# Hybrid encoder block with a mixture of experts: a slice-ordered copy of x2, and a row bound on the gathers and scatters

## The chip, the core and the metric

The kernel runs on one core of a Trainium2 chip. TensorE (PE in the rows) multiplies matrices, with a weight load (PEld) for the stationary operand of each product; VectorE (DVE), ScalarE (ACT) and GpSimd (POOL) work elementwise; SyncE (SP) issues transfers; sixteen DMA engines move data between HBM and the on-chip memory. The metric is the device time of one launch, the median of several runs, in microseconds (us).

## The reference

One encoder layer over 512 tokens of width 1024, all in float32:

```python
h = rmsnorm(x, norm_mix_w[l])
proj = h @ w_in[l]
...
merged = g_attn * (attn @ w_attn_o[l]) + g_ssd * (ssd @ w_ssd_o[l])
x = x + merged @ w_out[l]                     # called x2 below
h2 = rmsnorm(x, norm_ffn_w[l])
x = x + hierarchical_moe(h2, ...)
...
def hierarchical_moe(h, w_rg, b_rg, w_re, b_re, w1, w3, w2):
    p_group = softmax(t @ w_rg + b_rg); g_val, g_idx = top_k(p_group, 1)
    fine_sel = ...                            # the 4 expert logits of the group
    e_val, e_idx = top_k(softmax(fine_sel), 2)
    ...
    for e in range(16):
        y_e = (silu(t @ w1[e]) * (t @ w3[e])) @ w2[e]
        out = out + combine[:, e:e + 1] * y_e
```

Each token goes to one group of four experts and to two experts in it, so 1024 pairs of token and expert are to be computed. An expert has w1 and w3 of 1024 x 512 and w2 of 512 x 1024, 96 MB of weights over all sixteen.

## The kernel before

**Up to x2.** Input projection, attention, the two-way state-space part, the gates and the output projection come first. The last of it is `wout_mm`, after which `x2_add` (L1361) forms x2 in four blocks of 128 tokens, each in two halves. The sum's squares (`x2_sq`, L1364, ScalarE) give the norm's factor. For the router, `u_t` (L1369, TensorE) transposes a half block of x2, `u_out` (L1376, ScalarE) copies it out, `logits` (L1384, TensorE) multiplies it with the router's weights, `lg_copy` and `lg_sum` (L1387 to L1392) add the parts up, and `topk` (L1409 to L1444, VectorE) picks the experts. `pos_mm` and `base_mm` (L1446 to L1457) count the tokens ahead of each, which gives every pair of token and expert a slot.

**Slots.** Each expert has 96 slots, in three parts r of 32. The sixteen experts run in four rounds q, four experts (4j + q) at a time, so that a part of a round is 128 rows: 32 slots of each of four experts. `s_oh` (L1644) builds one-hot matrices of tokens against slots, `s_mm` multiplies them with a table of token numbers and factors, `s_ix` (L1663) turns the result into row numbers for the gathers, and `s_ti` (L1672 ff.) into factors and into row numbers for the scatters. An empty slot gathers row 0 and scatters to a spare row behind the 512 tokens, for which the output has 128 rows more.

**The first round's first part** isn't gathered. `oh_first` (L1473, VectorE) makes one-hots, and `pg_first` (L1480 to L1483) multiplies x2, as the stationary operand, with them: 24 products, for blocks t = 0, 1, 2 and for eight k. The slice k of x2 is every eighth column. `first_out` (L1703, L1706) puts the product into TH, the transposed tokens of the experts.

**The other eleven parts** are gathered by rows from h_d (called h2_d in the code), the copy of x2 in HBM that `h2_store` (L1400) writes; `gather` (L1685, GpSimd) fills GS or GX, `turn` (L1692, TensorE) transposes every eighth column at a time, `turned` (L1698, L1703) copies out.

**The experts.** `up_mm` (L1718) makes pu with w1 and pv with w3, `g_silu` and `g_mul` (L1741, L1745) join them, `turn` transposes, `down_mm` (L1726) multiplies with w2, `y_ev` (L1896, L1898) scales, `scatter` (L1748, GpSimd) adds the 128 rows of a part to the output in HBM. x2 itself was stored there first by `x2_store` (L1403). The phases run u0 v0 u1 w0 v1 u2 w1 v2 u3 w2 v3 w3 (u for w1, v for w3, w for w2, then the round). A part that would need more than 96 slots is done in an overflow loop, which these inputs don't enter.

**The weights** come as 192 loads of 512 KB (`eload`, L1750 to L1753, SyncE), in a fixed order, into 33 buffers: 21 of their own and 12 (EXu, EXx, EXr) that are made out of memory which other work leaves. A load waits in SyncE's queue until its buffer is free.

**What sets the order.** A planner in the program (class `Plan`) schedules all jobs of TensorE, VectorE, ScalarE, GpSimd and SyncE before the launch, by priorities, dependencies and prices that are written in the code, and the program is emitted in that order.

Of the kernel before, what the change touches and what calls it, by code (L numbers as in the profile page):

```python
# [217 lines left out]
def tile_block(ctx: ExitStack, tc: tile.TileContext, x, norm_mix_w, w_in, b_gate, q_norm_w, k_norm_w,  # L218
# [350 lines left out]
    spare = cp.tile([P, 1], F32, name="spare")  # L569
    tsb = cp.tile([P, P], BF16, name="tsb")  # L570

    def router_c():
# [903 lines left out]

    def pg_first(t, kb, js):
# [181 lines left out]
    def s_ix(nm, q, rs):  # L1659
# [3 lines left out]
        V.tensor_scalar(ix[q][:, a:b], pi_(nm)[:, a:b, 0], 0.0, None, op0=ALU.add)  # L1663
        V.tensor_tensor(ix[q][:, a:b], ix[q][:, a:b], pi_(nm)[:, a:b, 1], op=ALU.add)
    ix, ti, sx, ri = {}, {}, {}, {}

# [379 lines left out]
```

## Time and profile before

| | us |
|---|---|
| median of 3 runs | 672.26 (670.43 to 672.67) |
| profiled execution | 671.2 |
| its span in the profile | 669.4 |
| TensorE busy | 651.3 |
| VectorE busy | 321.5 |
| ScalarE busy | 240.7 |
| GpSimd busy | 83.0 |

The span is the time between the first and the last recorded work; the execution's own time holds some 2 us more around it. TensorE's clock was granted in full up to the last matmuls. The page shows shares of busy time over the whole span, and since the stages differ, the rows that follow are taken from single stages: the first-round products from 370 to 384 us, the experts from 384 to 657, and the last scatter. The columns are told with each group.

### The profile page before, as it was taken

What the parts mean: (1) busy time and instruction counts of PE and PEld (TensorE: products, weight loads), DVE (VectorE), ACT (ScalarE), POOL (GpSimd) and SP (SyncE); (2) the same over time, 40 slices, a digit from 0 to 9 for tenths busy, and PEclk for the clock granted to TensorE, in tenths of its full rate; (3) what the DMA queues carried; (4) which work ended last, traced back from release to release, by engine and by line L of the source; (5) the groups of instructions that cost most, each with busy time, mean ns of one, the idle gap of its engine ahead of it and who ended that gap; (6) DMA issues with size and microseconds to landing.
All of it is one profiled execution on the core that took longest, in us unless ns stands there. A gap on an engine that the chain in (4) does not pass through costs nothing. (4 is left out here: it accounts for less than half of the span.)

```text
span 669.4 us, 11417 instructions
## 1 busy us (share of the span) xinstructions
PE 651.3 (97%) x4616; PEld 401.0 (60%) x4618; DVE 321.5 (48%) x677; ACT 240.7 (36%) x441; POOL 83.0 (12%) x110
## 2 busy tenths in 40 slices
PE   7999999999999999999999999999999999999982
PEld 5888887777788888888877833443334333333320
DVE  4779868987698997566433580420112011001100
ACT  5444555777567778633442110001100110011100
POOL 5434100222000000000002020110010001000111
PEclk9999999999999999999999999999999999999997
DMA  8732632564221112698754579999999999999934
GB/s 287 183 86 44 179 94 66 141 205 127 64 64 32 32 33 64 206 324 318 285 187 175 204 224 317 419 418 418 406 366 386 418 398 373 386 417 386 368 89 65
DMA packets 79612, 154.85 MB, mean 231 GB/s; under 512 B 8696, under 2 KB 45060, under 8 KB 79556
## 3 DMA queue, kind: packets, MB, share of 16 engines
q1 hardware_dynamic: 70692, 131.27, 53.7%
q0 software_dynamic: 6800, 22.76, 12.7%
q8 instruction: 37, 0.61, 0.4%
q10 hardware_dynamic: 2064, 0.07, 0.2%
q14 instruction: 19, 0.16, 0.1%
HBM read 143.48 MB, written 10.58 MB: 230 GB/s over the span
## 5 line engine op out<-in xcount | busy, mean ns | idle before, releaser
L271 PE MATMUL b<-hTh,wc_hi 128*128 128x512 f32 x208 | 85.4, 410 | 0.0
L273 PE MATMUL b<-hTh,wc_lo 128*128 128x512 f32 x208 | 82.2, 395 | 0.0
L272 PE MATMUL b<-hTl,wc_hi 128*128 128x512 f32 x208 | 82.2, 395 | 0.0
L1718 PE MATMUL pu<-u,TH 128*32 128x512 f32 x600 | 74.5, 593 | 0.0
L1726 PE MATMUL py<-w,GS 128*32 128x512 f32 x456 | 71.5, 592 | 1.7 <-DMA w<-in_w_dram 1.7
L1718 PE MATMUL pv<-v,TH 128*32 128x512 f32 x456 | 69.0, 593 | 0.0
L1896 DVE TENSOR_SCALAR YS<-py,ti 128x512 f32<-128x512 f32 x12 | 9.0, 751 | 116.8 <-PE py L1726 116.4
L271 PEld LDWEIGHTS b<-hTh,wc_hi 128*128 128x128 f32 x208 | 39.1, 188 | 10.2 <-issue 1.5
L669 DVE TENSOR_TENSOR wc_lo<-wc_r,wc_hi 128x1024 fp32r<-128x1024 f32 x34 | 41.5, 1223 | 7.7 <-ACT wc_hi L665 7.5
L1698 ACT ACTIVATE GS<-pts 128x512 f32<-128x512 f32 x12 | 6.6, 597 | 106.9 <-PE pts L1692 106.9
L273 PEld LDWEIGHTS b<-hTh,wc_lo 128*128 128x128 f32 x208 | 39.1, 188 | 9.4
L665 ACT ACTIVATE wc_hi<-wc_r 128x1024 fp32r<-128x1024 f32 x34 | 35.8, 1056 | 24.4 <-PE b L272 14.9
L1718 PEld LDWEIGHTS pu<-u,TH 128*32 128x32 f32 x600 | 20.5, 110 | 39.1 <-issue 37.0
L272 PEld LDWEIGHTS b<-hTl,wc_hi 128*128 128x128 f32 x208 | 39.2, 188 | 7.7
L1726 PEld LDWEIGHTS py<-w,GS 128*32 128x32 f32 x456 | 19.4, 110 | 39.0 <-issue 33.2
L1748 POOL DMA_INDIRECT out_dram<-YS,sx x12 | 18.7, 1559 | 190.1 <-DVE YS L1896 132.4
L1718 PEld LDWEIGHTS pv<-v,TH 128*32 128x32 f32 x456 | 18.6, 110 | 29.7 <-issue 27.9
L1703 DVE TENSOR_TENSOR TH<-ptt,nfc 128x512 f32<-128x512 f32 x21 | 13.2, 684 | 46.3 <-PE ptt L1692 46.3
L1898 ACT ACTIVATE YS<-py,ti 128x512 f32<-128x512 f32 x12 | 8.3, 688 | 69.4 <-PE py L1726 69.1
L1745 DVE SCALAR_TENSOR_TENSOR YS<-pv,ri,YS 128x512 f32<-128x512 f32 x8 | 6.0, 751 | 56.1 <-PE pv L1718 55.9
L1718 PE MATMUL pv<-EXr,TH 128*32 128x512 f32 x108 | 32.1, 593 | 0.0
L1741 ACT ACTIVATE YS<-pu,ri 128x512 f32<-128x512 f32 x8 | 5.5, 688 | 62.8 <-PE pu L1718 56.3
(367 smaller groups left out, 1393.3 us busy)
## 6 DMA issues: line engine op xcount, KB each, us to landing
u<-in_w_dram SPq DMA_DIRECT2D x50, 512.0 KB
v<-in_w_dram SPq DMA_DIRECT2D x38, 512.0 KB
w<-in_w_dram SPq DMA_DIRECT2D x38, 512.0 KB
wc_r<-in_w_in_dram SPq DMA_DIRECT2D x26, 512.0 KB
EXu<-in_w_dram SPq DMA_DIRECT2D x24, 512.0 KB
EXr<-in_w_dram SPq DMA_DIRECT2D x22, 512.0 KB
EXx<-in_w_dram SPq DMA_DIRECT2D x20, 512.0 KB
x<-in_x_dram SPq DMA_DIRECT2D x8, 512.0 KB
```

Source lines behind the costliest of these rows:

```text
L271: T.matmul(ps, lhsT=lh, rhs=rh, start=first, stop=False)
L272: T.matmul(ps, lhsT=lh, rhs=rl, start=False, stop=False)
L273: T.matmul(ps, lhsT=ll, rhs=rh, start=False, stop=last)
L665: A.activation(t_["w", i][0], t_["raw", i], AF.Copy)
L669: V.tensor_tensor(l_, t_.pop(("raw", i)), h_.bitcast(F32), op=ALU.subtract)
L1698: A.activation(sT_(g[2]), i, AF.Copy)
L1703: V.tensor_tensor(o, i, nfc[:, k0:k0 + 4].unsqueeze(2).to_broadcast([P, 4, P]), op=ALU.mult)
L1718: T.matmul(t_["p", x_, q, r][js, :], lhsT=T_(q, r)[:, k, js], rhs=t_["raw", x_, q, k // 2, j][:, k % 2, :], start=k == 0, stop=k == KD - 1)
L1726: T.matmul(t_["p", h, q, r][js, :], lhsT=sT_(r)[:, k, js], rhs=t_["raw", "w", q, k, j].rearrange("p a n -> p (a n)")[:, int(h) * 512:(int( ...
L1748: G.indirect_dma_start(out, bass.IndirectOffsetOnAxis(ap=sx[q][:, r:r + 1], axis=0), y_buf(r), None, compute_op=ALU.add)
L1896: V.tensor_scalar(o, i, w_, None, op0=ALU.mult)
L1898: A.activation(o, i, AF.Copy, scale=w_)
```

## The change

- `u_w` is new: ScalarE copies x2 into a buffer us of the same size with the columns put in slice order (slice k contiguous), eight copies of 128 x 512.
- `pg_first` takes its stationary operand from us, in contiguous slices; the planner's price of a pair of products goes from 0.51 to 0.29.
- `h2_store` stores us instead of x2, so that gathered rows are in slice order, and `turn` reads them contiguously.
- The table of token numbers has NONE = 4096 taken off, and `s_ix` adds it back, so that an empty slot has a row number above 511. Gathers and scatters get a bound of 511 for the row, beyond which a row is left out. The scatters use the gathers' row numbers; the spare rows, their numbers and the output's extra rows are gone.
- `clear` is new: three memsets on GpSimd of the buffers into which the gathers write, ahead of the first gather.
- The planner gets other priorities (`oh_first` earlier, the second round's slots later), and the buffers that are made out of freed memory are others: us takes the place of two of them, and the two halves of each lp come in.

```diff
-        c[:, C_TC + 2 * t + 1] = t * P
+        c[:, C_TC + 2 * t + 1] = t * P - NONE
...
+    def u_w(t, nh):
+        A.activation(us(t).rearrange("n (k p) -> n k p", k=KD)[:, :, nh * 64:nh * 64 + 64],
+                     x2(t)[:, nh * 512:(nh + 1) * 512].rearrange("n (p k) -> n k p", k=KD), AF.Copy)
+
     def h2_store(t):
-        G.dma_start(h2_d[t * P:(t + 1) * P, :], x2(t))
+        G.dma_start(h2_d[t * P:(t + 1) * P, :], us(t))
...
-            T.matmul(t_["pg", kb][:, j * P:(j + 1) * P], lhsT=x2(t).rearrange("n (p k) -> n k p", k=KD)[:, kb * 4 + j, :],
+            T.matmul(t_["pg", kb][:, j * P:(j + 1) * P], lhsT=us(t)[:, (kb * 4 + j) * P:(kb * 4 + j + 1) * P],
                      rhs=oh0()[:, t, :], start=False, stop=(t, j) == (NT - 2, 3))
...
+        w_ = job("act", 0.65, lambda: u_w(t, nh), [j_] + j_x2, prio=prio + (2 if t < NT - 1 or nh == 0 else 8))
...
-        j_ = job("dve", 0.17, lambda t=t: oh_first(t), [j_slot[t]], prio=PGP)
+        j_ = job("dve", 0.17, lambda t=t: oh_first(t), [j_slot[t]], prio=-1000)
...
+    def clear(r):
+        G.memset(g_buf(r), 0.0)
...
-        V.tensor_scalar(ix[q][:, a:b], pi_(nm)[:, a:b, 0], 0.0, None, op0=ALU.add)
+        V.tensor_scalar(ix[q][:, a:b], pi_(nm)[:, a:b, 0], float(NONE), None, op0=ALU.add)
...
-        st += [lambda: V.tensor_copy(fx, pi_(nm)[:, :, 0]),
-               lambda: V.tensor_tensor(fx, fx, pi_(nm)[:, :, 1], op=ALU.add),
-               lambda: V.reduce_sum(own, w_.rearrange("p r j i -> p r i j"), axis=AX.X),
-               lambda: V.reduce_sum(ti[q], own[:, :, 0:3], axis=AX.X),
-               lambda: V.scalar_tensor_tensor(fx, fx, spare[:, 0:1], own[:, :, 3], op0=ALU.subtract, op1=ALU.mult),
-               lambda: V.tensor_scalar(sx[q], fx, spare[:, 0:1], None, op0=ALU.add)]
+        st += [lambda: V.reduce_sum(own, w_.rearrange("p r j i -> p r i j"), axis=AX.X),
+               lambda: V.reduce_sum(ti[q], own[:, :, 0:3], axis=AX.X)]
...
-        G.indirect_dma_start(g, None, h2_d, bass.IndirectOffsetOnAxis(ap=i, axis=0))
+        G.indirect_dma_start(g, None, h2_d, bass.IndirectOffsetOnAxis(ap=i, axis=0), bounds_check=S - 1, oob_is_err=False)
...
-        src = g_buf(g[2]).rearrange("n (p k) -> n k p", k=KD) if g[0] == "t" else s_buf(g[2]).rearrange("n (k p) -> n k p", k=4)
+        src = g_buf(g[2]).rearrange("n (k p) -> n k p", k=KD) if g[0] == "t" else s_buf(g[2]).rearrange("n (k p) -> n k p", k=4)
...
-        G.indirect_dma_start(out, bass.IndirectOffsetOnAxis(ap=sx[q][:, r:r + 1], axis=0), y_buf(r), None, compute_op=ALU.add)
+        G.indirect_dma_start(out, bass.IndirectOffsetOnAxis(ap=ix[q][:, r:r + 1], axis=0), y_buf(r), None, bounds_check=S - 1,
+                             oob_is_err=False, compute_op=ALU.add)
...
+    for i, h, after in ((0, 1, [j_ra]), (0, 0, uts), (1, 0, uts + pgs + [j_w5, j_tab]), (1, 1, uts + pgs + [j_w5, j_tab])):
+        job("any", 0.0, lambda i=i, h=h: ebufs.append(
+            lambda nm, dt=F32, pat=None, **kw: lp[i][:, h * 1024:(h + 1) * 1024].rearrange(pat, **kw)), after, free=["e"], lat=0.0)
     for i in range(2):
-        more(g8, "EXx%d" % i, [j for t in (2 * i, 2 * i + 1) for n in range(2) for j in js[t][n]] + j_st[2 * i:2 * i + 2]
-             + j_h2[2 * i:2 * i + 2] + pgt[2 * i] + (pgt[1] if i == 0 else []))
-    more(a8, "EXr0", uts + [j_rooms])
-    more(a8, "EXr1", uts + pgs + [j_w5, j_tab, j_rooms])
+        more(g8, "EXu%d" % i, j_h2[2 * i:2 * i + 2] + (pgt[0] + pgt[1], pgt[2])[i])
...
-        o = (700, at["u", 0] + 8, at["v", 0] + 38, at["v", 0] + 39)[q]
+        o = (700, at["u", 0] + 32, at["v", 0] + 38, at["v", 0] + 39)[q]
```

On TensorE, the end of the first products before: pg_3644 and pg_3675 are the two halves of the products, x_0 and x_1 the blocks of x2, plt the router's sums, and pu the first up-product.

```order
L1480 MATMUL pg_3675<-zb,onb 128x512
L1482 MATMUL pg_3675<-lp_3257,x_0_3296 128x128 x4
L1384 MATMUL plt<-lp_3256,wr 32x128 x4
...
L1457 MATMUL plt<-mk,onb 128x16
L1482 MATMUL pg_3644<-lp_3257,x_0_3296 128x128 x4
L1392 MATMUL plt<-sel,lp_3257 128x20 x2
L1482 MATMUL pg_3675<-lp_3257,x_0_3296 128x128 x4
L1482 MATMUL pg_3644<-lp_3257,x_1_3299 128x128 x4
L1482 MATMUL pg_3675<-lp_3257,x_1_3299 128x128 x4
L1718 MATMUL pu_0_3742<-u_0_0_2920,TH_3650 32x512
```

The same place after the change, where the products are pg_3649 and pg_3669 and read us.

```order
L1488 MATMUL pg_3669<-lp_3255,us_3383 128x128 x2
L1371 MATMUL ph_3_1_3678<-cst,x_1_3298 128x128 x4
L1488 MATMUL pg_3669<-lp_3255,us_3383 128x128 x2
L1488 MATMUL pg_3649<-lp_3255,us_3383 128x128 x4
L1488 MATMUL pg_3669<-lp_3255,us_3383 128x128 x4
...
L1386 MATMUL plt<-lp_3254,wr 32x128 x4
L1488 MATMUL pg_3649<-lp_3255,us_3421 128x128 x2
L1394 MATMUL plt<-sel,lp_3255 128x20 x2
L1488 MATMUL pg_3649<-lp_3255,us_3421 128x128 x2
L1488 MATMUL pg_3669<-lp_3255,us_3421 128x128 x4
L1726 MATMUL pu_0_3746<-u_0_0_2918,TH_3655 32x512
```

More of the products now stand ahead of the last block's logits (L1386, L1384 before), and eight instead of sixteen behind them; nothing else changed places there.

On VectorE, between the third block's slots and the eviction of the first products (TH) before:

```order
L1460 TENSOR_SCALAR low<-plt 128x16
L1644 TENSOR_TENSOR oh_149<-cst,slot 128x384
L1644 TENSOR_TENSOR oh_150<-cst,slot 128x384
L1644 TENSOR_TENSOR oh_148<-cst,slot 128x384
L1406 SCALAR_TENSOR_TENSOR lp_3257<-plt,rs_141,prm 128x20
L1473 TENSOR_TENSOR lp_3257<-cst,slot 128x128
L1431 TENSOR_REDUCE lp_3257<-lp_3257 128x5
...
L1436 TENSOR_TENSOR lp_3257<-lp_3257 128x20
L1703 TENSOR_TENSOR TH_3650<-pg_3644,nfc 128x512
```

And after:

```order
L1467 TENSOR_SCALAR low<-plt 128x16
L1480 TENSOR_TENSOR lp_3255<-cst,slot 128x128
L1654 TENSOR_TENSOR oh_148<-cst,slot 128x384
L1654 TENSOR_TENSOR oh_149<-cst,slot 128x384
L1654 TENSOR_TENSOR oh_147<-cst,slot 128x384
L1413 SCALAR_TENSOR_TENSOR lp_3255<-plt,rs_140,prm 128x20
L1711 TENSOR_TENSOR TH_3655<-pg_3649,nfc 128x512
L1438 TENSOR_REDUCE lp_3255<-lp_3255 128x5
```

The third one-hot for the products (L1480, L1473 before) moved ahead of the three 128x384 one-hots, and the eviction into TH moved ahead of the last block's choice of experts.

On SyncE, the loads of the second half of v0 (w3 of the first round) before, by buffer:

```order
L1753 DMA v_0_2_3347<-in_w_dram 128x1024
L1347 DMA wt_3_r<-in_w_out_dram 128x2x512
L1753 DMA EXu_3363<-in_w_dram 128x1024 x2
L1753 DMA EXu_3387<-in_w_dram 128x1024 x2
L1753 DMA v_1_3_3418<-in_w_dram 128x1024
L1753 DMA v_2_0_3460<-in_w_dram 128x1024
L1753 DMA EXr_3716<-in_w_dram 128x1024 x2
L1753 DMA EXx_3740<-in_w_dram 128x1024 x2
L1753 DMA EXx_3777<-in_w_dram 128x1024 x2
L1753 DMA EXr_3838<-in_w_dram 128x1024 x2
```

And after, where EXx_3571 and EXu_3718 lie in the blocks of x2 and wait for the x2 stores, EXx_3762 and EXu_3814 lie in us and wait for the h2 stores and the products:

```order
L1349 DMA wt_3_r<-in_w_out_dram 128x2x512
L1762 DMA v_0_3_3354<-in_w_dram 128x1024
L1762 DMA v_1_0_3392<-in_w_dram 128x1024
L1762 DMA v_1_1_3458<-in_w_dram 128x1024
L1762 DMA EXx_3571<-in_w_dram 128x1024 x2
L1762 DMA EXu_3718<-in_w_dram 128x1024 x2
L1762 DMA EXx_3762<-in_w_dram 128x1024 x2
L1762 DMA lp_3254<-in_w_dram 128x1024
L1762 DMA EXu_3814<-in_w_dram 128x1024 x2
L1762 DMA lp_3255<-in_w_dram 128x1024 x2
```

Four loads (EXu_3363, EXu_3387) needed no late release before; now EXu_3718 and the seven loads behind it wait for the last block's stores or the products.

## Rows read from the trace of the kernel before

**Rows 1.** The page, busy us by engine, with share of span and instructions.

```profile
PE 651.3 (97%) x4616; PEld 401.0 (60%) x4618; DVE 321.5 (48%) x677; ACT 240.7 (36%) x441; POOL 83.0 (12%) x110
```

**Rows 2.** Windows of the expert stage: busy us (instructions) by engine, clock, DMA share, GB/s.

```profile
450.00:475.00 25.00, 25.00 (x237) 7.83 (x240) 1.71 (x3) 2.22 (x4) 1.78 (x2) 1.00 1.03 418
```

**Rows 3.** Waits of SyncE's queue, 400 to 640 us: total us, times, longest.

```profile
SPq L1753 <- PE pu L1718: 22.3, 7, 19.2
```

**Rows 4.** Timeline of TensorE near the end: start, us, instruction, count, idle before and releaser.

```profile
634.84 1.90 PE L1726 MATMUL py<-EXu,GS 128*32 128x512 f32 x16
637.04 1.04 PE L1726 MATMUL py<-w,GS 128*32 128x512 f32 x2 [0.30 <-DMA w<-in_w_dram]
639.52 1.05 PE L1726 MATMUL py<-w,GS 128*32 128x512 f32 x2 [1.43 <-DMA w<-in_w_dram]
640.76 1.04 PE L1726 MATMUL py<-EXr,GS 128*32 128x512 f32 x2 [0.20 <-DMA EXr<-in_w_dram]
642.00 0.62 PE L1726 MATMUL py<-EXr,GS 128*32 128x512 f32 x1 [0.19 <-SPq L2009]
```

**Rows 5.** Windows after the last matmul, columns as in rows 2.

```profile
661.00:665.00 4.00, 0.00 (x0) 0.00 (x0) 0.00 (x0) 0.00 (x0) 0.00 (x0) 0.64 0.86 131
665.00:669.40 4.40, 0.00 (x0) 0.00 (x0) 0.00 (x0) 0.00 (x0) 0.00 (x0) 0.50 0.00 0
```

**Rows 6.** Timeline of TensorE, first-round products to first transposes of gathered rows.

```profile
377.42 0.52 PE L1392 MATMUL plt<-sel,lp 128*128 128x20 f32 x4
377.78 5.99 PE L1482 MATMUL pg<-lp,x 128*128 128x128 f32 x24
383.70 0.64 PE L1718 MATMUL pu<-u,TH 128*32 128x512 f32 x4
...
399.10 0.71 PE L1692 MATMUL ptt<-cst,GS 128*128 128x128 f32 x4
```

**Rows 7.** Groups of weight loads over the span: busy us, mean ns, idle before.

```profile
L1482 PEld LDWEIGHTS pg<-lp,x 128*128 128x128 f32 x48 | 11.8, 334 | 0.0
L1392 PEld LDWEIGHTS plt<-sel,lp 128*128 128x128 f32 x16 | 2.3, 191 | 0.3
L1692 PEld LDWEIGHTS ptt<-cst,GS 128*128 128x128 f32 x56 | 6.8, 193 | 3.4 <-issue 3.4
L1692 PEld LDWEIGHTS pts<-cst,YS 128*128 128x128 f32 x32 | 3.4, 141 | 4.2 <-issue 2.5 <-DVE YS L1745 1.7
```

**Rows 8.** Timeline of TensorE: four contiguous transposes, eight strided ones, the next product.

```profile
440.05 0.60 PE L1692 MATMUL pts<-cst,GS 128*128 128x128 f32 x4
440.48 1.05 PE L1692 MATMUL ptt<-cst,GS 128*128 128x128 f32 x8
441.47 1.06 PE L1718 MATMUL pu<-u,TH 128*32 128x512 f32 x8
```

**Rows 9.** Timeline of VectorE beside the first products.

```profile
376.19 1.50 DVE L1644 TENSOR_TENSOR oh<-cst,slot 128x384 bf16<-128x384 f32 x3
...
381.89 0.69 DVE L1703 TENSOR_TENSOR TH<-pg,nfc 128x512 f32<-128x512 f32 x1 [2.20 <-PE pg L1482]
```

**Rows 10.** Timeline of ScalarE, one half block of x2: its squares, then the logits' copy.

```profile
364.22 0.63 ACT L1364 ACTIVATE lp<-x 128x512 bf16<-128x512 f32 x1 [1.20 <-DVE x L1361]
...
365.28 0.60 ACT L1376 ACTIVATE lp<-ph 128x512 f32<-128x512 f32 x1 [0.33 <-PE ph L1369]
```

**Rows 11.** Timeline of TensorE: the logits that read this copy.

```profile
366.56 0.43 PE L1384 MATMUL plt<-lp,wr 128*32 128x128 f32 x8
```

**Rows 12.** Timeline of GpSimd: the last store of x2 and the first gather.

```profile
372.09 0.53 POOL L1403 DMA_DIRECT2D out_dram<-x  x1
...
389.53 1.26 POOL L1685 DMA_INDIRECT GS<-h_d,ix  x1 [16.33 <-issue]
```

**Rows 13.** DMA issues by line: count, KB each, median us from issue to landing.

```profile
out_dram<-x POOLq DMA_DIRECT2D x4, 512.0 KB, 4.8
GS<-h_d,ix POOLq DMA_INDIRECT x7, 6.2
```

More of the change, by code (lines that the diff above doesn't have):

```diff
@@ L69 @@
 OFF = 2048
+NONE = 4096
 TG = ((0, 2), (2, 3), (3, 4))
@@ L1765, in tile_block @@
     j_rooms = job("any", 0.0, rooms, wo_all, lat=0.0)
[L1766 removed]
+    uts = [js[t][n][i] for t in range(NT) for n in range(2) for i in (2, 3)]
     pgs = pgj[0] + pgj[1]
     for i in range(2):
[L1769 removed]
+        more(g8, "EXx%d" % i, [j for t in (2 * i, 2 * i + 1) for n in range(2) for j in js[t][n]] + j_st[2 * i:2 * i + 2])
+    for i, h, after in ((0, 1, [j_ra]), (0, 0, uts), (1, 0, uts + pgs + [j_w5, j_tab]), (1, 1, uts + pgs + [j_w5, j_tab])):
+        job("any", 0.0, lambda i=i, h=h: ebufs.append(
+            lambda nm, dt=F32, pat=None, **kw: lp[i][:, h * 1024:(h + 1) * 1024].rearrange(pat, **kw)), after, free=["e"], lat=0.0)
     for i in range(2):
[L1771 to L1774 removed]
+        more(g8, "EXu%d" % i, j_h2[2 * i:2 * i + 2] + (pgt[0] + pgt[1], pgt[2])[i])
     phases = [("u", 0), ("v", 0), ("u", 1), ("w", 0), ("v", 1), ("u", 2), ("w", 1), ("v", 2), ("u", 3), ("w", 2), ("v", 3), ("w", 3)]
@@ L1786, in tile_block @@
                     [j_rq] + ([last["e"]] if "e" in last else []), ["e"], prio=1000 + len(jw), lat=DLAT)
+    jcl = [job("pool", 0.9, lambda r=r: clear(r), [j_rooms], prio=PL + 40 + r) for r in (1, 2, 0)]
     def sl_jobs(q):
-        o = (700, at["u", 0] + 8, at["v", 0] + 38, at["v", 0] + 39)[q]
+        o = (700, at["u", 0] + 32, at["v", 0] + 38, at["v", 0] + 39)[q]
         rs = list(range(NR))
@@ L1810, in step @@
             tis[i][1]()
-        for i in range(NR + 7):
-            j_ = jri[q, i] = job("dve", 0.09, lambda i=i: step(i), [j_], free=["tp"] if i == NR + 6 else [], prio=o + 6 * (q == 0))
+        for i in range(NR + 3 + (q == 0)):
+            j_ = jri[q, i] = job("dve", 0.09, lambda i=i: step(i), [j_], free=["tp"] if i == NR + 2 + (q == 0) else [], prio=o + 6 * (q == 0))
         jti[q] = [k_, j_]
@@ L1815, in sl_jobs @@
             if (q, r) != (0, 0):
-                k_ = job("pool", 1.03, lambda r=r: gather(g_buf(r), ix[q][:, r:r + 1]), [jx, j_rooms] + j_h2 + jg_[-1:],
+                k_ = job("pool", 1.03, lambda r=r: gather(g_buf(r), ix[q][:, r:r + 1]), [jx, j_rooms] + j_h2 + jcl + jg_[-1:],
                          ["G"], prio=o + r)
@@ L1905, in tile_block @@
     turn_jobs(v_[0] + 6, ("tp", "tp", "sc", "sc"), [("t", 0, r, kb) for kb in range(2) for r in (1, 2)])
-    for q in (2, 3):
+    for q in (1, 2, 3):
         jpi[q][3].append(jtu["t", 0, 1, 0])
@@ L2006, in xround @@
             A.activation(y_[:N, hs], product(ex[2], sT, 4, hs, "sc", "pyx%d" % h)[:N], AF.Copy, scale=fxx[:N, 1:2])
-        G.indirect_dma_start(out, bass.IndirectOffsetOnAxis(ap=sxx[:N, 0:1], axis=0), y_[:N], None, compute_op=ALU.add)
+        G.indirect_dma_start(out, bass.IndirectOffsetOnAxis(ap=ixx[:N, 0:1], axis=0), y_[:N], None, bounds_check=S - 1,
+                             oob_is_err=False, compute_op=ALU.add)
     with tc.If(tot > 0):
```

33 lines of the change are left out of this document (14 added, 19 removed).

## The prediction

> **What bounds the kernel now.** I read the page first, then the windows of the expert stage, then the end of the timeline. TensorE is busy in 651.3 of 669.4 us [rows 1], so time is saved only where TensorE's records come closer together, where it waits, or after its last matmul. The expert stage runs at TensorE's pace and at the DMA engines' limit together: from 450 to 475 us TensorE is busy throughout (237 records in 25 us, 0.106 us each) while the DMA share is 1.03 [rows 2]. SyncE, which issues the weight loads, stood still for 19.2 us on the first-round products [rows 3], that is, all buffers were full then, and the stock of loaded weights shrinks from there to the end. At 634.84 it is used up: TensorE's next 22 records take until 642.00, 7.16 us, where 22 x 0.106 = 2.3 would do. So 4.8 us are lost to late weights, and the releasers named are loads [rows 4]. After the last matmul comes the last scatter: its data move from 661 to 665 at a DMA share of 0.86, and after that nothing moves until 669.4 [rows 5].
>
> **The first products (shorter).** The 48 records of the first round's products with x2 as weights come 24 in 5.92 us, from 377.78 to 383.70, or 247 ns each [rows 6]. What paces them is the weight load, 334 ns against 191 for the same shape read contiguously in the logit sum [rows 7]; the stride of eight elements is what differs. With contiguous slices I price a record by the transposes of rows 8: four contiguous ones take 440.48 - 440.05 = 0.43, or 108 ns, eight strided ones 441.47 - 440.48 = 0.99, or 124 ns. I take 115; the low bound is the logit sum's spacing, 0.36/4 = 90 ns [rows 6]. That gives 48 x (247 - 115) = 6.3 us, with 5.9 and 7.5 as bounds. Part of it goes back: between the third slot numbers and the first up-product VectorE has a chain of its own, three one-hots in 1.50 and the eviction of the products in 0.69 [rows 9], which the products used to cover. TensorE now reaches it sooner. I count 0.9 us of waiting for it (0.9 to 1.5 in the bounds). The up-products then start at 383.70 - 5.4 = 378.3. **5.4 us (4.4 to 6.6).**
>
> **The eight copies.** ScalarE writes x2 by slices in eight 128x512 activations. The nearest row reads x2 contiguously and takes 0.63 [rows 10]. Seven of the eight stand ahead of the copy that feeds the logits (L1376). There ScalarE has 0.33 us idle, and 366.56 - 365.88 = 0.68 us lie between that copy's end and the logits on TensorE, which does other matmuls meanwhile [rows 10, 11]. About 1.0 us is therefore free at each of the seven places, and a copy of 0.63 fits. Its strided read could be dearer. Scaled by the load rows it is 0.63 x 193/141 = 0.86, or at worst 0.63 x 334/141 = 1.5 [rows 7], which would cost 7 x 0.5 = 3.5 us. I take 0, since a transpose's load of the same stride is the milder case and a copy has no such overlap to lose; the 3.5 stays in the range. The Trainium skill, "SBUF — State Buffer", section "Door 1: The DMA port swizzle", speaks against these copies: it says that SBUF is read in lines of 16 bytes and that striding beyond four fp32 pays a penalty on each access. The load rows agree with it, no row before shows it on ScalarE, and by it the copy would lie above 0.63.
>
> **The transposes of gathered tokens.** Stored in slice order, h2 comes back from the gathers contiguous. The 88 strided transposes (56 of GS, 32 of GX; [rows 7] has the first) go from 124 to 108 ns [rows 8]: 88 x 16 ns = **1.4 us** (0 to 1.4, if something else paces them).
>
> **Rows that are left out.** By the reference's routing 1024 of the 1536 slots hold a token. The last part of each round (r = 2, slots 64 to 95) holds only 15, 12, 11 and 13 tokens of 128; the first two hold 99 to 128. A full scatter keeps the DMA engines 4.0 x 0.86 = 3.4 us busy [rows 5]. What a part-filled one costs depends on how its rows are dealt to the 16 engines, which no row shows: eight rows each before, in 4 us, so 0.5 us a row. Filled rows are neighbours (partitions 64 to 75). If they are spread evenly, one engine gets one row and nine tenths of a scatter is gone; if they stay together by eights, one engine still has eight and nothing is gained. I take the middle, four on the busiest. Then three scatters within the stage give 3 x 1.7 = 5.1 us, and three gathers of as many bytes, counted at a weight load's price (512 KB at 418 GB/s [rows 2], 1.25 us), give 3 x 0.6 = 1.9, together 7.0. Needed are the 4.8 of the end plus the 1.4 by which TensorE gets ahead through the transposes. The earlier start needs nothing, since TensorE's first releases start the refill and move with it [rows 3]. So the late weights vanish: **4.8 us** (2.4 to 4.8 in my case; 0 is the first rival). The last scatter (13 tokens) moves its data in 2.0 instead of 4.0 us: **1.9 us** (0 to 3.4). The Trainium skill, "DMA: Bandwidth & Descriptors", section "Anatomy of one DMA — SWDGE (gpsimd) path", prices a transfer by bytes, 2.0 us plus bytes by 436 GB/s; an estimate from it is 3.2 us full and 2.1 with 13 rows, so 1.1 saved and a time of 659.6. The trace does not agree, as this scatter's data alone take 4 us.
>
> **Hidden or nil.** Three memsets of 128x1024 on GpSimd stand ahead of the first gather, before which GpSimd is idle 16.33 us [rows 12]; uncovered they would cost about 1 us each. VectorE drops the tail-row arithmetic (a few operations of 0.1 to 0.2 us), none of it awaited. The order on TensorE ahead of the products is unchanged, so nothing is earned or lost before 370 us.
>
> **The sum** is 5.4 + 1.4 + 4.8 + 1.9 = 13.5 us. The profiled execution took 671.2, 1.1 under the median of 672.26; it goes to 657.7, and the median to 672.26 - 13.5 = **658.8 us**.
>
> **Rivals.**
> (B) *The DMA limit stays.* Empty slots still cost their descriptors, or the filled neighbours stay on one engine. Then the 1.4 and 4.8 are lost to weights that come no earlier, the last scatter keeps its 4 us, and only the start's 5.4 remains: 666.9. For it: the rows of r = 2 are neighbours. Against it: the page's shares count busy engines, and a row that is not sent leaves nothing to count.
> (C) *New waits in the first round.* Four pairs of w3 pieces, before loaded early, now wait in SyncE's queue for the store of the last x2 (372.09 + 4.8 = 376.9 [rows 12, 13]) or for the last products. The transposes that follow their use began at 399.10, now 393.7 [rows 6], and the last quarter of the products that read them, 16 records, begins 1.7 earlier at 392.0. Eight loads at 1.25 take 10 us, and the store's 4.8 for as many bytes leaves up to 3.5 of latency: they are there between 386.9 and 390.4. The first gather, issued at 389.53 [rows 12] and now up to 5.4 earlier as its slots are, say at 386, lands 6.2 later by the median [rows 13], at 392.2, against the 393.7. Margins of 1.5 us, so a wait of 1 to 4 is possible: 659.8 to 662.8.
> (D) *Slower.* The strided copies on ScalarE cost far more than the rows suggest. Each microsecond beyond 1.0 is paid seven times on the way to the logits, since TensorE runs out of other matmuls there. Past 1.0 + (13.5 + 2.0)/7 = 3.2 us a copy the kernel is slower than before by more than can be told; at 3.6 us it takes 658.8 + 18 = 677. For it: a strided read is the one new thing there. Against it: the dearest strided row costs 2.4 times its contiguous twin, not 5 times.
>
> **How the numbers follow.** My case has 0.67, B 0.15, C 0.14, D 0.04. About 0.3% (2.0 us) is what a measurement of this kernel can tell from no change. The best sum of bounds is 6.6 + 1.4 + 4.8 + 3.4 = 16.2, or 656.1; the lowest run before lies 1.8 under its median, so I put the low end at 654.0. Upwards, 3.5 for dear copies gives 662.3, C ends at 662.8, and my own case with all its low bounds (4.4 + 0 + 2.4 + 0 = 6.8) at 665.5; that is the high end. Outside lie B and D, 0.19. Faster than before by over 0.3% are my case, B and C with 0.95 (a little off for a B whose start is eaten up); within it 0.01; slower 0.04.
>
> **What would show it right or wrong.** The products' weight loads at about 190 ns and the first up-product near 378; ScalarE's copies under 1 us, with no new wait of TensorE before 372; strided transposes gone to loads of 141; no wait of TensorE for weights after 600 us and a DMA share below 1 somewhere before it; last matmul near 645; from the last scatter's start to the end about 8 us instead of 10. A DMA share still at 1.03 up to 630 with a wait for weights behind it is B. Waits of TensorE for EX loads or for GS near 385 to 395 are C. What would make the whole forecast wrong is a copy above 3 us, or a stage that is paced by a resource that I have not seen.

## The result and the profile after

The changed kernel takes 661.6 us (median of 4 runs, 661.1 to 662.42) against 671.38 of the kernel before in the same series (670.43 to 672.67). The ratio is 0.986, interval 0.9844 to 0.9876, so 9.8 us are gained where 13.5 were predicted. The median lies 2.8 us above the predicted 658.8 and inside the range. The profiled executions give spans of 659.9 and 669.4 us.

Engine line of the page of the changed kernel (against [rows 1]), then two windows of it, with columns as in [rows 2]:

```profile
PE 643.1 (97%) x4616; PEld 394.0 (60%) x4618; DVE 320.5 (49%) x662; ACT 248.5 (38%) x449; POOL 86.8 (13%) x113
```

```profile
450.00:475.00 25.00, 25.00 (x240) 7.62 (x236) 2.11 (x3) 4.13 (x6) 0.80 (x1) 1.00 1.03 418
620.00:630.00 10.00, 10.00 (x92) 3.32 (x88) 2.25 (x3) 1.79 (x3) 1.55 (x1) 1.00 0.64 223
```

TensorE is busy 8.2 us less with the same 4616 records. In the middle of the expert stage nothing is new: DMA share 1.03 at 418 GB/s, as in [rows 2]. From 620 to 630 us the share is down to 0.64, and TensorE no longer waits there: the weights are all loaded.

To see where the time went I cut the span at seven events that every kernel here has, and compare the pieces: px is the first matmul of the output projection, which feeds x2, pg the first product of the first round, pu the first up-product, pts the last transposes, ys0 and ys2 the scaling of the first and the last part of the last round, sc the start of the last scatter. In us, each from the timeline of that kernel:

| piece | before | after | difference |
|---|---|---|---|
| start to px | 317.35 | 317.40 | +0.05 |
| px to pg | 53.21 | 53.75 | +0.54 |
| pg to pu | 13.14 | 7.92 | -5.22 |
| pu to pts | 248.81 | 248.57 | -0.24 |
| pts to ys0 | 10.62 | 6.15 | -4.47 |
| ys0 to ys2 | 13.73 | 13.73 | 0 |
| ys2 to sc | 2.48 | 2.96 | +0.48 |
| sc to the end | 10.06 | 9.42 | -0.64 |
| sum | 669.4 | 659.9 | -9.50 |

The start lies between 315.2 and 319.1 in the kernels below, none of which changes anything there, so it is left out where kernels are compared below by pieces; the times contain it. In seven of them (e1, e1b, e2, e3, e5, e8, e9) the granted clock of the profiled execution is 0.50 for 3.4 or 6.8 us between 10 and 19 us, in the others it is not.

**The first products.** Timeline of TensorE of the changed kernel (start, us, instruction, count, idle before and releaser), then the tiles' weight loads (count: least/median/most ns):

```profile
373.14 2.40 PE L1488 MATMUL pg<-lp,us 128*128 128x128 f32 x20
376.64 0.71 PE L1488 MATMUL pg<-lp,us 128*128 128x128 f32 x4 [0.62 <-DVE lp L1480]
377.56 1.58 PE L1488 MATMUL pg<-lp,us 128*128 128x128 f32 x12
379.07 3.64 PE L1726 MATMUL pu<-u,TH 128*32 128x512 f32 x32
```

```profile
L1488 PEld LDWEIGHTS pg<-lp,us x48: 186/192/200, 370.9 to 378.8; 128*128 128x128 f32 x48
L1700 PEld LDWEIGHTS ptt<-cst,GS x56: 138/141/143, 394.2 to 510.8; 128*128 128x128 f32 x56
```

A weight load of these products takes 192 ns instead of 334 [rows 7]. The last twelve products come in 1.51 us, 126 ns each instead of 247 [rows 6]. TensorE waits 0.62 us for the third one-hot, on VectorE, and the up-products start at 379.07 instead of 383.70.

**The copies.** Timeline of ScalarE (against [rows 10]), the copies as a group, and the logits on TensorE that wait:

```profile
365.43 1.17 ACT L1403 ACTIVATE us<-x 128x512 f32<-128x512 f32 x1
366.50 0.58 ACT L1378 ACTIVATE lp<-ph 128x512 f32<-128x512 f32 x1
```

```profile
L1403 ACT ACTIVATE us<-x x8: 1127/1186/1283, 337.5 to 372.5; 128x512 f32<-128x512 f32 x8
```

```profile
339.25 0.43 PE L1386 MATMUL plg<-lp,wr 128*32 128x128 f32 x8 [0.26 <-ACT lp L1378]
```

A copy takes 1.19 us, almost twice the 0.63 of a contiguous read [rows 10]. It shows as one wait of 0.26 us, and 0.54 us in the piece from px to pg. The Trainium skill, "SBUF — State Buffer", section "Door 1: The DMA port swizzle", has SBUF read in 16-byte lines and a penalty for strides beyond four fp32; the trace agrees, and gives the size that the Trainium skill does not: a factor of 1.9 for a stride of eight.

**The end.** Chain of waits of the changed kernel (start, us, what), the scatters on GpSimd, and the windows after the last one:

```profile
643.07 6.63 DMA out_dram<-YS,ix
```

```profile
643.07 1.55 POOL L1756 DMA_INDIRECT out_dram<-YS,ix  x1 [5.41 <-DMA out_dram<-YS,ix]
650.48 1.55 POOL L1756 DMA_INDIRECT out_dram<-YS,ix  x1 [5.86 <-DMA out_dram<-YS,ix]
```

```profile
652.00:655.00 3.00, 0.00 (x0) 0.00 (x0) 0.00 (x0) 0.00 (x0) 0.03 (x1) 0.50 0.16 21
655.00:659.90 4.90, 0.00 (x0) 0.00 (x0) 0.00 (x0) 0.00 (x0) 0.00 (x0) 0.50 0.01 2
```

The last scatter's data now move at a share of 0.16 and are through by 655, but the span ends 4.9 us later, as it ended 4.4 us after the data before [rows 5]. What runs until then is a DRAIN instruction of GpSimd's queue. The row of the kernel before and that of the changed one (count: least/median/most ns, first and last start; the longest is the one meant, and the first to start):

```profile
L2042 POOLq DRAIN  x3: 46/109/6587, 662.0 to 669.2; - x3
```

```profile
L2050 POOLq DRAIN  x3: 46/109/5954, 653.1 to 659.7; - x3
```

In both kernels it begins 2.67 us after the scatter's start and the span ends 0.8 us behind it, so the 0.64 us of the table are the drain's, 6.59 us before and 5.95 after. And the last scatter now waits for the one before it, which landed at 649.69.

### The profile page after: what moved, and what is told of

The parts are those of the page before. It is cut to its first block, busy times and chain, and to the rows that moved or that the text cites. A ratio compares the mean times of both kernels' runs of the same rounds, so it can differ in the third digit from the quotient of the medians.

```text
span 659.9 us, 11444 instructions
## 1 busy us (share of the span) xinstructions
PE 643.1 (97%) x4616; PEld 394.0 (60%) x4618; DVE 320.5 (49%) x662; ACT 248.5 (38%) x449; POOL 86.8 (13%) x113
## 2 busy tenths in 40 slices
DMA packets 79613, 150.67 MB, mean 228 GB/s; under 512 B 9720, under 2 KB 46084, under 8 KB 79556
## 4 chain that ended last, share of the span: by engine, by line
PE 91%; DMA 5%; ACT 1%; issue 1%; DVE 0%; SPq 0%; POOL 0%; POOLq 0%; ACTq 0%
PE pu L1726 13%; PE pv L1726 13%; PE py L1734 11%; PE b L272 10%; PE b L274 10%; PE b L273 10%; PE px L272 2%; PE ppt L1153 2%; PE px L273 2%; PE px L274 2%; DMA out_dram<-YS,ix 2%; DMA kv_r<-in_w_in_dram 2%; PE ptt L1700 2%; PE py L1006 1%; PE sc L1132 1%; PE po L1174 1%
## 5 line engine op out<-in xcount | busy, mean ns | idle before, releaser
L1726 PE MATMUL pu<-u,TH 128*32 128x512 f32 x600 | 69.3, 594 | 0.0
L1726 PE MATMUL pv<-v,TH 128*32 128x512 f32 x456 | 63.4, 593 | 0.0
L1734 PE MATMUL py<-w,GS 128*32 128x512 f32 x456 | 63.0, 592 | 0.0
L1756 POOL DMA_INDIRECT out_dram<-YS,ix x12 | 18.7, 1558 | 185.9 <-DVE YS L1908 122.3
L1734 PEld LDWEIGHTS py<-w,GS 128*32 128x32 f32 x456 | 17.9, 110 | 34.3 <-issue 32.2
L1734 PE MATMUL py<-EXx,GS 128*32 128x512 f32 x132 | 37.8, 593 | 0.0
L1726 PE MATMUL pv<-lp,TH 128*32 128x512 f32 x120 | 37.4, 592 | 0.0
```

The lines of the kernel that those rows point to most:

```text
L1726: T.matmul(t_["p", x_, q, r][js, :], lhsT=T_(q, r)[:, k, js], rhs=t_["raw", x_, q, k // 2, j][:, k % 2, :], start=k == 0, stop=k == KD - 1)
L1734: T.matmul(t_["p", h, q, r][js, :], lhsT=sT_(r)[:, k, js], rhs=t_["raw", "w", q, k, j].rearrange("p a n -> p (a n)")[:, int(h) * 512:(int( ...
L1756: G.indirect_dma_start(out, bass.IndirectOffsetOnAxis(ap=ix[q][:, r:r + 1], axis=0), y_buf(r), None, bounds_check=S - 1, oob_is_err=False, ...
```

## The experiments

All ratios are against the kernel before, timed in the same series (medians 670.46 to 671.06). The bound on the rows can be taken out of the gathers (an empty slot's index is masked to a real row, and all 128 rows are fetched) and out of the scatters (an empty slot goes to one of 128 spare rows behind the output). That gives kernels with one half of the change, or with the copy alone.

### Bound taken out of both, and out of one

**e1_all_rows**: both. **e3_scatter_bound**: gathers fetch all rows, scatters stay bounded. **e4_gather_bound**: the reverse.

```diff
+spare = cp.tile([P, 1], F32, name="spare")                                    # e1, e4
+V.tensor_scalar(gx[q][:, a:b], ix[q][:, a:b], S - 1, None, op0=ALU.bitwise_and) # e1, e3
+V.tensor_scalar(sx[q][:, a:b], ix[q][:, a:b], spare[:, 0:1], None, op0=ALU.min) # e1, e4
-gather(g_buf(r), ix[q][:, r:r + 1])                                           # e1, e3
+gather(g_buf(r), gx[q][:, r:r + 1])
-G.indirect_dma_start(out, ...ix[q][:, r:r + 1]..., bounds_check=S - 1, oob_is_err=False, ...)
+G.indirect_dma_start(out, ...sx[q][:, r:r + 1]..., compute_op=ALU.add)        # e1, e4
```

> The changed kernel, but gathers and scatters move all 128 rows again (an empty slot gathers row 0 and scatters to a spare row); copies, slices and buffers stay. Theory (the bound takes the late weights away): the 4 MB come back, TensorE waits for weights near the end for 4 to 6 us again, and the last scatter is 0.6 longer: 666 to 668 us. Rival (the loads come in time because their buffers were rearranged): no wait, 662.2.

> The changed kernel with the bound on the scatters alone; gathers read all 128 rows (row 0 for an empty slot). Theory (half of the bytes left out are enough, since the loads now end over 10 us before TensorE's last product): no wait for weights, 661.6 to 662. Rival (both are needed): 663 to 665.

> The changed kernel with the bound on the gathers alone; scatters write all 128 rows (spare rows for empty slots). Theory (gathers give back 2.1 MB, 5 us at 418 GB/s, about what is needed; the last scatter is 0.6 longer): 662.2 to 663.5. Rival (an accumulating scatter costs more DMA time a byte than a gather, so that the wait returns): 664 to 667.

Measured: e1 676.98 us, ratio 1.0092 [1.0059, 1.0124], slower than the kernel before. e3 669.45, 0.9973 [0.9956, 0.999]. e4 668.83, 0.9956 [0.994, 0.9973]. That was more than the bound could account for, and the windows showed a second difference. Expert stage of e1, columns as in [rows 2]:

```profile
450.00:475.00 25.00, 25.00 (x237) 7.65 (x240) 1.27 (x3) 2.69 (x4) 1.44 (x2) 1.00 1.02 408
```

The same DMA share moves 408 GB/s instead of 418. The small new tiles had pushed most of the weight buffers (all but EXu and EXx) to other addresses in SBUF: by 288, 128 and 160 bytes in e1, e3 and e4. So these three can be compared with each other and with a shifted version of the changed kernel (e9, below), but not with the kernel itself.

### The same with the buffers in place

**e1b_all_rows_aligned**: e1, but the spare rows' numbers lie in a tile that was there, and the shift is 256 bytes. **e8_before_shifted**: the kernel before with 128 bytes more ahead of the buffers. **e9_after_shifted**: the changed kernel, likewise.

```diff
-spare = cp.tile([P, 1], F32, name="spare")                # e1b, against e1
-msk = cp.tile([P, 4], F32, name="msk")
+msk8 = cp.tile([P, 8], F32, name="msk")
+msk, spare = msk8[:, 0:4], msk8[:, 4:5]

-spare = cp.tile([P, 1], F32, name="spare")                # e8, against before
+spare = cp.tile([P, 33], F32, name="spare")[:, 0:1]

-msk = cp.tile([P, 4], F32, name="msk")                    # e9, against after
+msk = cp.tile([P, 36], F32, name="msk")[:, 0:4]
```

> As e1_all_rows, but the added small tiles leave the weight buffers at a multiple of 256 bytes, as in both kernels (in e1, e3 and e4 the tiles had moved them to 32 or 128 past one, and loads ran at 408 instead of 418 GB/s between 450 and 475 us). Theory (the place of the buffers sets that rate; the bound takes the late weights away): 418 GB/s again, a wait for weights near the end of 5 to 6 us instead of 11, so 667 to 672 us. Rival (the rate has to do with the added operations or the chip): 677 as e1.

> The kernel before with nothing changed but a tile that is 128 bytes longer, so that the weight buffers lie at 128 past a multiple of 256 bytes. Theory (the place sets the rate): 408 to 410 instead of 418 GB/s, 2.4% of the 224 us of loading, so the wait near the end grows by 5 and the time goes to 676 us. Rival (place is of no account): 671.

> The changed kernel with nothing changed but a tile that is 128 bytes longer, so that the weight buffers lie at 128 past a multiple of 256 bytes, as in e8_before_shifted. Theory (loads slow to 408 GB/s, but with the bound they end early enough): 661.6 to 662.5, no wait for weights. Rival (loads still bound the stage): 665, with a wait near the end.

Measured: e1b 672.61, 1.0018 [1.0001, 1.0036]. e8 674.53, 1.0048 [1.0033, 1.0063]. e9 665.56, 0.9919 [0.9902, 0.9936]. The same window in e1b, e8 and e9, in this order:

```profile
450.00:475.00 25.00, 25.00 (x236) 7.70 (x238) 1.58 (x3) 2.38 (x4) 1.75 (x2) 1.00 1.03 417
```

```profile
450.00:475.00 25.00, 25.00 (x232) 8.78 (x232) 2.48 (x4) 2.06 (x3) 1.87 (x2) 1.00 1.03 409
```

```profile
450.00:475.00 25.00, 25.00 (x240) 7.54 (x232) 0.45 (x1) 4.13 (x6) 0.00 (x0) 1.00 1.03 408
```

So the shift alone costs the kernel before 4.1 us in medians (674.53 against 670.46; 3.2 by the ratio), the changed one 4.0 (665.56 against 661.6), and e1 4.4 against e1b (5.0 by the ratios). In the profiled executions 2.4 us of it (e8 against before) and 2.9 (e9 against after) lie between pts and ys0, where the weights are late. I had expected none from e9, since its weights seemed to come with time to spare; they don't.

With the address settled, e1b is the copy without the bound: **672.6 us, no faster than the kernel before**. The bound is worth 672.61 - 661.6 = 11.0 us (10.6 by the ratios), more than the whole change. Where e1b loses against after: 3.93 us from pu to pts, 7.70 from pts to ys0. The profiled execution of e1b is the slowest of its ten (674.41), so the pieces add up to somewhat more than the medians differ by. Waits of TensorE in e1b (us in total, times, longest), the first transposes of GX there, and TensorE's windows behind them:

```profile
PE ptt L1709 <- DMA GX<-h_d,gx: 2.1, 1, 2.1
PE py L1743 <- DMA w<-in_w_dram: 1.9, 1, 1.9
```

```profile
397.60 0.63 PE L1709 MATMUL ptt<-cst,GX 128*128 128x128 f32 x4 [2.09 <-DMA GX<-h_d,gx]
399.63 2.95 PE L1735 MATMUL pu<-u,TH 128*32 128x512 f32 x16
```

```profile
398.00:400.00 2.00, 2.00 (x15) 1.50 (x16) 0.95 (x2) 1.14 (x4) 0.00 (x0) 0.59 0.00 0
400.00:402.00 2.00, 2.00 (x16) 0.39 (x8) 0.43 (x1) 0.00 (x0) 0.00 (x0) 0.56 0.00 0
402.00:404.00 2.00, 2.00 (x32) 0.78 (x28) 0.91 (x5) 0.00 (x0) 0.16 (x1) 1.00 0.00 0
```

The first gather into GX, with all its rows, lands too late: its transposes follow 8.65 us after the issue (388.95), in the changed kernel 6.45 (388.22 and 394.67). TensorE stands for 2.1 us, and behind that the granted clock is 0.59 and 0.56, the lower of its two levels (1.2 GHz) for most of 4 us, which costs another 1.7 (0.41 and 0.44 of two stretches of 2 us). The sum is 3.8 of the 3.93. e1 (wait of 1.8) and e3 (2.1) show the same drop. In e2, e5, e6 and e9, with 0.7 to 1.1 us of the same wait, the clock stays at 1.00 behind it, and so it does in the changed kernel, which has no wait there:

```profile
394.18 0.66 PE L1700 MATMUL ptt<-cst,GS 128*128 128x128 f32 x4
394.67 0.60 PE L1700 MATMUL ptt<-cst,GX 128*128 128x128 f32 x4
396.07 0.64 PE L1726 MATMUL pu<-u,TH 128*32 128x512 f32 x4
```

The late weights follow from the loads. The kernels of this table stop loading with full buffers and issue the same 159 weight loads afterwards. From SyncE's timeline, the time from the first of them to the last one's issue, and the piece in which TensorE pays (in e1 the granted clock is 0.50 there from 637.1 to 640.5 us):

| kernel | buffers | rows left out of | first load | 159 loads take | pts to ys0 |
|---|---|---|---|---|---|
| before | in place | nothing | 404.74 | 224.1 | 10.62 |
| after | in place | both | 400.25 | 218.5 | 6.15 |
| e1b | in place | nothing | 404.85 | 227.9 | 13.85 |
| e9 | shifted | both | 402.21 | 224.0 | 9.05 |
| e3 | shifted | scatters | 403.94 | 228.5 | 12.06 |
| e4 | shifted | gathers | 398.37 | 228.8 | 14.71 |
| e1 | shifted | nothing | 404.53 | 233.2 | 17.36 |

First and last row of that for the changed kernel:

```profile
400.25 16.07 SPq L1762 DMA_DIRECT2D u<-in_w_dram  x15
...
618.47 0.33 SPq L1762 DMA_DIRECT2D EXx<-in_w_dram  x1
```

Leaving rows out of the scatters shortens the loading by 4.7 us (e1 to e3), out of the gathers by 4.4 (e1 to e4), out of both by 9.2 (e1 to e9) or 9.3 (e1b to after). The page's DMA totals say part of why: 154.85 MB before, 150.67 after. Of these 4.18 MB 3.1 fall between the first of the 159 loads and the last one's issue, by the packets in the traces (8.91 MB of gathered and scattered rows there in e1b, 5.78 in the changed kernel); the rest belongs to the first gathers and the last scatters. At 418 GB/s 3.1 MB are 7.5 us of the 9.3. Where the other 1.8 come from is open. The new order of loads and gathers gives some back: e1b needs 3.8 us more than before for the same loads and rows. Part of that is visible: from 400 to 405 us, while the loads stood, the kernel before moved 120 GB/s (the next gathers' rows), e1b nothing, and its gathers fell among the loads, 8.91 MB of rows there against 7.85, which is 2.5 us at 418 GB/s. The rest is open.

### The copy without the slice order

**e2_plain_copy**: x2 is copied as it lies; the products and the transposes keep their strides.

```diff
-A.activation(us(t).rearrange("n (k p) -> n k p", k=KD)[:, :, nh * 64:nh * 64 + 64],
-             x2(t)[:, nh * 512:(nh + 1) * 512].rearrange("n (p k) -> n k p", k=KD), AF.Copy)
+A.activation(us(t)[:, nh * 512:(nh + 1) * 512], x2(t)[:, nh * 512:(nh + 1) * 512], AF.Copy)
...
-lhsT=us(t)[:, (kb * 4 + j) * P:(kb * 4 + j + 1) * P]
+lhsT=us(t).rearrange("n (p k) -> n k p", k=KD)[:, kb * 4 + j, :]
...
-src = g_buf(g[2]).rearrange("n (k p) -> n k p", k=KD) ...
+src = g_buf(g[2]).rearrange("n (p k) -> n k p", k=KD) ...
```

> The changed kernel, but the copy keeps the column order of x2, so that the first products and all 88 transposes are strided as before; order, buffers and bounds stay. Theory (slices give 5.2 us in the products and 0.3 in the transposes; the copy that reorders costs TensorE 0.5): 661.6 + 5.2 + 0.3 - 0.5 = 666.6, with copies of 0.63 instead of 1.18. Rival (the transposes gain the 1.4 of the forecast): 667.7. Rival (the products were not paced by their weight loads): 662.

Measured: 669.09 us, 0.9958 [0.9943, 0.9974]. The slice order is worth 669.09 - 661.6 = 7.5 us in medians, 6.6 by the ratios, and 6.6 by the pieces without the start. By pieces against after: the products take 13.91 instead of 7.92, pu to pts 250.21 instead of 248.57, and px to pg 53.21 instead of 53.75. So the contiguous copies are free, the 0.54 us is the price of the stride. Of the 1.64 from pu to pts, 0.68 is a wait for the gather into GX:

```profile
402.33 0.69 PE L1699 MATMUL ptt<-cst,GX 128*128 128x128 f32 x4 [0.68 <-DMA GX<-h_d,ix]
```

Another 0.2 is the clock's: in this execution it was granted at 0.50 from 382.7 to 386.1 us, over the last products and the first up-products, after a wait of 0.62 us for the third one-hot and four products (behind the same wait it stays at 1.00 in the changed kernel); the first four up-products are followed by the next after 0.67 us instead of 0.43. (On the twelve products ahead of them, 261 ns each against 247 in the kernel before, it costs another 0.2.) What is left, 0.7 us or less, is all that 88 strided transposes can cost.

### The price and the place of the copies

**e6_copy_twice**: every copy is made twice. **e5_copy_gpsimd**: GpSimd makes them. **e10_true_price**: the scheduler is told 1.18 us for a copy where it was told 0.65, so its order may change.

```diff
+A.activation(us(t)..., x2(t)..., AF.Copy)                 # e6: the call a second time

-A.activation(us(t)..., x2(t)..., AF.Copy)                 # e5
+G.tensor_copy(us(t)..., x2(t)...)
-w_ = job("act", 0.65, lambda: u_w(t, nh), ...)
+w_ = job("pool", 1.2, lambda: u_w(t, nh), ...)

-w_ = job("act", 0.65, lambda: u_w(t, nh), ...)            # e10
+w_ = job("act", 1.18, lambda: u_w(t, nh), ...)
```

> The changed kernel with each of the eight copies done twice, so 2.36 us in place of 1.18 at each place. Theory (about 1.1 us is free at each of seven places and the rest is paid, as the forecast's slower rival has it): 7 x 1.2 = 8 us more, 668 to 670. Rival (TensorE has enough other matmuls there): 662 to 664.

> The changed kernel with its eight copies on GpSimd instead of ScalarE. Theory (the copies of 1.18 cost TensorE 0.5 us ahead of the products, no more): 661.1. Rival (GpSimd is slower at it, and the last copy comes late for the products and for the stores that free buffers): 662 to 666.

> The changed kernel with the planner's price of a copy at 1.18, as measured, in place of 0.65; the first copies then stand behind what the logits need. Theory (the 0.5 us that TensorE lost before the products is got back): 661.1. Rival (another order of the copies costs as much elsewhere): 661.6 to 662.5.

Measured: e6 668.27, 0.9955 [0.9937, 0.9974]; e5 663.35, 0.9881 [0.9852, 0.991]; e10 661.64, 0.9869 [0.9852, 0.9885]. Waits of TensorE in e6:

```profile
PE plg L1386 <- ACT lp L1378: 3.9, 3, 1.5
PE plt L1386 <- ACT lp L1378: 3.2, 3, 1.1
```

The second copies add eight times 1.19 = 9.5 us to ScalarE. The piece from px to pg grows by 6.97, and these waits sum to 7.1 against 0.3. TensorE waits at six places ahead of the logits, not at the prediction's seven, for 1.0 to 1.5 us each where 1.19 were added: with the single copy the room there is about used up. So rival D's arithmetic (about 1 us free at each place, paid in full beyond that) holds here, at six places; only the price it needs, 3.2 us a copy, was far from the 1.19.

On GpSimd a copy takes as long, and the last store of h2, which GpSimd issues, comes later (at 375.82 instead of 373.95); TensorE then waits for the gather. The piece from px to pg is 53.85 there, so the 0.54 us don't come back either; TensorE waits for VectorE in it, twice for 0.3 us. From e5, the copies and that wait:

```profile
L1403 POOL COPY us<-x x8: 1101/1180/2107, 337.0 to 373.9; 128x512 f32<-128x512 f32 x8
```

```profile
PE ptt L1700 <- DMA GX<-h_d,ix: 1.1, 1, 1.1
```

e10 orders other work around the copies and comes out at the same time: the wait for the logits' copy is gone, and others for VectorE (0.4 and 0.2 us) are there. No version here beats the changed kernel.

### What the last scatter costs

**e7_no_last_scatter**: the last scatter is left out.

```diff
+if (q, r) == (NQ - 1, NR - 1):
+    return
```

> The changed kernel without its last scatter (round 3, part 2; those 13 rows are left out of the output). Theory (what follows the last landing is fixed, about 5 us of the 9.4 from the last scatter's start to the end): the end comes about 5 us after the landing of the scatter before, 649.7, so 655 and 5 us saved. Rival (the tail is work of its own that starts only when TensorE is done): 657 to 659.

Measured: 655.47 us (one run), span 653.7. Without it VectorE's last scaling ends at 649.2 and the scatter before lands at 649.9, and the span still goes on to 653.7 with almost nothing moving:

```profile
651.00:652.00 1.00, 0.00 (x0) 0.00 (x0) 0.00 (x0) 0.00 (x0) 0.00 (x0) 0.50 0.02 8
```

So the last scatter costs 661.6 - 655.47 = 6.1 us although it carries 13 rows. Most of that is not its data. Here the drain begins at 645.25, 2.67 us after the scatter before started, and ends 3.0 us after that one landed; in the changed kernel it begins at 653.15, because the last scatter waits for the landing of the one before, and takes its 5.95 from there. The traces of all the kernels fit one reading, which no run tests by itself: the drain ends 3.0 us after the last landing, but no sooner than 5.95 us after its own start. The first holds where the last scatter has all its 128 rows (before, e1, e1b, e4, e8) and in e7, the second wherever it has 13.

## Why the prediction came out as it did

**Start, 5.4 predicted, 5.22 measured: right.** The loads fell to 192 ns as forecast, and VectorE's chain gave back about what was counted (0.62 us of waiting). Net of the copies the up-products start 4.6 us sooner.

**Copies, 0 predicted, 0.54 paid: mis-sized.** The prediction took the contiguous 0.63, on the ground that a transpose's load is the milder case. 1.19 was measured, between its 0.86 and its 1.5. The free 1.0 us at each place hid all but the 0.54. Had the prediction taken the value in the middle of its bounds, it would have seen that the room was filled, which e6 shows: the next microsecond is paid six times.

**Transposes, 1.4 predicted, 0.24 measured (0.7 at most, by e2): mis-sized.** The loads did fall from 193 to 141 ns, but the transposes are not paced by them. Sixteen in the changed kernel, and the rows of the kernel before that I should have used, with sixteen strided ones and eight contiguous ones:

```profile
414.77 1.97 PE L1700 MATMUL ptt<-cst,GS 128*128 128x128 f32 x16
416.66 0.62 PE L1726 MATMUL pv<-v,TH 128*32 128x512 f32 x2
```

```profile
419.25 2.05 PE L1692 MATMUL ptt<-cst,GS 128*128 128x128 f32 x16
421.24 0.63 PE L1718 MATMUL pv<-EXu,TH 128*32 128x512 f32 x3
...
505.53 1.09 PE L1692 MATMUL pts<-cst,YS 128*128 128x128 f32 x8
506.46 0.60 PE L1692 MATMUL pts<-cst,GS 128*128 128x128 f32 x4
```

Strided they go 1.99/16 = 124 ns, contiguous 1.89/16 = 118 after and 0.93/8 = 116 before. The 108 and 124 of the prediction [rows 8] were not taken alike: behind its four contiguous ones came more transposes, while the time of its eight strided ones holds the step to the next product, 0.2 us. From record to record the traces show 112 ns strided and 109 contiguous, and 0.21 against 0.17 us for the first step of a piece. 88 x 7 ns = 0.6 is what was there to gain.

**Late weights, 4.8 predicted, 4.47 measured: right in sum, by two errors that cancel.** All weights come in time, and leaving out rows is the reason, as predicted: without it (e1b) the piece is 7.70 us longer. But the relief was not 7.0. It is 9.3 (e1b to after). The scatters gave 4.7 where it had 5.1, the gathers 4.4 where it had 1.9. That nearly all the empty slots lie in the last parts was right (461 of 512, by its own counts); but it took half of a gather's bytes as saved, where nine tenths are left out: three gathers without 116 rows of 4 KB each are 3.4 us at 418 GB/s. And the new order costs 3.8 of loading, which it did not have. Net 5.5, for 7.0 predicted; but only what came late counts, and the margin was enough.

**"The earlier start needs nothing" held only with the bound.** In the changed kernel the first load follows the first up-product by 400.25 - 379.07 = 21.2 us, before by 404.74 - 383.70 = 21.0: it does move with TensorE. But in e1b, with the same early start, the late GX and the lower clock behind it take the start back, and the first load is at 404.85. So rival B was mispriced: without the relief not 666.9 but 672.6.

**Rival C was closer than its 0.14.** Its wait for the first gather into GX is absent from the changed kernel, where that gather lands at 394.1, only 0.6 us before its transposes. It is there with 1.8 to 2.1 us in e1, e1b and e3, which gather all rows, and with 0.7 to 1.1 in e2, e5, e6 and e9, which leave rows out. So leaving rows out shortens the gather but does not by itself bring it in time; that the changed kernel has no wait at all is a margin of 0.6 us, and in part luck. Against e1b it saves 3.9 us which the prediction, in which the bound only relieves the end, did not count.

**Last scatter, 1.9 predicted, 0.16 measured: the end does not follow its data.** The data shrank about as priced: from its start to its landing the scatter takes 4.64 us (650.48 to 655.12) instead of 6.27 (659.34 to 665.61), 1.63 less. But the prediction took the time behind the landing as fixed, and what ends last is GpSimd's drain, which is only 0.64 shorter: 5.95 us, 3.98 of them after the landing, where it was 3.00 before. And 0.48 goes back, because the scatter waits for the one before: its rows were scaled by 649.09, that one landed at 649.69. The prediction overlooked that scatters run one after another, each with 6 us from start to landing. The Trainium skill, "DMA: Bandwidth & Descriptors", section "Anatomy of one DMA — SWDGE (gpsimd) path", gave the prediction's other estimate, 1.1 us saved. The trace has 1.63 us to the landing and 0.64 to the end, so it does not agree.

In sum 5.22 - 0.54 + 0.24 + 4.47 + 0.16 - 0.05 (the start of the run) = 9.50 of 13.5. Of the missing 4.0 us, 1.7 lie in the last scatter, 1.2 in the transposes, 0.5 in the copies.

## What to carry over

Price a stage that runs at the DMA limit by the bytes that it moves, all of them and only those within it; 3.1 MB left out of the loading gave 9.3 us here, of which 418 GB/s account for 7.5. A transfer that is just in time can cost more than it is late by: the first gather late by 2.1 us cost 3.9, as the clock fell behind the wait. Before shortening what comes last, look at what the end of the program waits for. And when an experiment adds a tile, look at where it pushes the others, before a difference of 4 us is read as the edit's.

## What the hardware showed beside

**The place of the weight buffers.** Where the 21 own buffers begin at a multiple of 256 bytes in SBUF, the stretch from 450 to 475 us runs at 416 to 418 GB/s (before, after, e1b, e2, e5, e6, e7, e10, with shifts of 0 and 256 bytes). Where they lie 32, 128 or 160 bytes beyond one (e1, e3, e4, e8, e9), it runs at 408 to 409, with the same DMA share of 1.02 to 1.03. That is 2.4%, and it stretches 159 loads from 218.5 to 224.0 us (after to e9). e2, which is otherwise another kernel than after, is at the full rate:

```profile
450.00:475.00 25.00, 25.00 (x236) 8.73 (x232) 2.48 (x4) 2.06 (x3) 1.98 (x2) 1.00 1.03 417
```

That a load is slow because its own target is off such a multiple is not shown, and one thing speaks against it. EXu and EXx lie 224 bytes beyond a multiple in every kernel, and 37 of the changed kernel's 159 loads go there. Their packets of 4096 bytes, counted off in the order of the loads, take 161 ns on average in it, as the others do; in e9 they take 162, the others 163. So the whole stream is slower or faster together, and what in the shift does it is open.

The Trainium skill, "DMA: Bandwidth & Descriptors", section "How a descriptor splits into AXI transactions", says that a descriptor is split into transactions of 256 bytes, and that one which doesn't start at a multiple of 256 has its first transaction start at the boundary below. An estimate from the Trainium skill's page, 17 transactions for 4096 bytes instead of 16, is 418 x 16/17 = 393 GB/s. The measured 408 agrees in direction, not in size, and by that rule the loads into EXu and EXx would be slow in every kernel, which they are not.

**The end of the program.** GpSimd's drain and 0.8 us behind it end every kernel here. With a last scatter of 128 rows (before, e1, e1b, e4, e8) the drain ends 3.0 us after the landing; with one of 13 rows (after, e2, e3, e5, e6, e9, e10) it takes 5.95 us and ends 3.7 to 4.1 after it.
